# Batched matrix product: one buffer in place of two for the cast weights and the transposed x, and x cast by row pairs

## The chip, the cores and the metric

The kernel runs on one core of one Trainium2 chip. The metric is the device time of one execution in microseconds; the comparison is between medians of several executions. A core has a matrix engine (TensorE, PE in the profile, with its weight loads as PEld), three engines for elementwise work (VectorE or DVE, ScalarE or ACT, GpSimd or POOL), and SyncE (SP), which here issues all transfers. Transfers between device memory and on-chip memory (SBUF) are carried by 16 DMA engines. TensorE writes its products to a separate accumulation memory, PSUM, from which VectorE or ScalarE copies them.

## What is computed

```python
def setup_inputs():
    b1, b2, m, k, n = 8, 16, 256, 512, 384
    return {
        "x": np.random.randn(b1, b2, m, k).astype(np.float32),
        "weight": np.random.randn(b1, b2, k, n).astype(np.float32),
    }

def reference(x, weight):
    return np.matmul(x, weight).astype(np.float32)
```

These are 128 independent products of a 256 x 512 matrix with a 512 x 384 matrix, in and out as float32. The kernel multiplies in bfloat16 and accumulates in float32. Each number of x, of the weights and of the output crosses the memory interface once: 167.77 MB are read and 50.33 MB written.

## The kernel before

The 128 products are taken in 32 groups of four (`G = 4`, `NG = 32`). The names below are those of the code.

**Layout.** The 1024 rows of x of one group lie on 128 partitions, eight rows to a partition (`R = 8`), so that each of the four products owns 32 partitions. The rows are handled in four row pairs (`T = 4`, index `q`), each being one row pair of every partition.

**Stages of one group.** Each engine has its own program, and they meet only at counting semaphores.

1. SyncE loads x (2048 KB, `load`, lines 97 to 104) and the weights in two halves (1536 KB each, lines 105 to 114).
2. ScalarE casts x from float32 to bfloat16 and reorders it (`cast_x`, line 131), two instructions of 2048 elements per partition. `x_cast` counts.
3. TensorE transposes the cast x (`multiply`, line 168), sixteen 128 x 128 transposes, four for each row pair, into one of four PSUM buffers `pt`. `t_made` counts row pairs.
4. VectorE casts the weights to bfloat16 (`prepare`, line 149) into `w_bf`, eight instructions on 64 partitions, two for each of the four products. `w_cast` counts.
5. VectorE copies the transposed x of each row pair from `pt` to `x_t` (line 155). `t_copied` counts row pairs.
6. TensorE multiplies (line 182): for each row pair 32 products of shape 128 x 32 by 128 x 384, four of which use different column strips of the array. They go to one of two PSUM buffers `po`. `p_made` counts row pairs.
7. ScalarE copies each row pair from `po` to `out_sb` (`copy_out`, line 196). `o_copied` counts.
8. SyncE stores the group (1536 KB, `store`, line 122).

**Order and buffers.** The order on every engine is written out by hand. TensorE does all transposes of a group, then all of its products, and then the transposes of the next group. VectorE does the eight casts of the weights and then the four copies of the transposed x. ScalarE casts the x of the next group between the second and the third output copy of the present one (`step`). SyncE loads group n + 4 in program order ahead of the store of group n, but the load of x of a group waits until the x of two groups before is cast (`XS = 2`), and a load of weights until those of two groups before are cast (`w_sb` has four halves). There are two buffers of `x_t` (`TS = 2`), and `w_bf` has eight places, for two groups (`WBS = 2 * G`), and one buffer of the cast x (`BS = 1`). The wait at the head of `prepare`,

```python
e.wait_ge(p_made, n * T + (BIAS - T))
```

lets VectorE start group n once the products of group n - 2 are done: since `p_made` starts at `BIAS`, a count of `n * T + BIAS` would mean that all groups up to n - 1 are done. In the same way `o_copied` lets the products of a row pair start once the row pair two before it is copied out (`PO = 2`).

**Loops.** VectorE and TensorE run loops with two groups in the body, ScalarE and SyncE with four.

Of the kernel before, what the change touches and what calls it, by code (L numbers as in the profile page):

```python
# [9 lines left out]


@with_exitstack
def kernel(
# [6 lines left out]
    nc = tc.nc  # L20
# [5 lines left out]
    KO = K // P  # L26
# [13 lines left out]
    G = 4  # L40
    C = P // G
    R = G * M // P
    T = R // 2
    D = 2
    S = 2
    HP = P // D
    NG = B // G

    XS, WS, OS = 2, 2 * G // D, 4
    BS, TS, WBS = 1, 2, 2 * G  # L50
    PT, PO = 4, 2

    LAG = 4
# [3 lines left out]
    def sbuf(name, shape, dtype, n):  # L57
        return [
            ctx.enter_context(nc.sbuf_tensor(f"{name}{s}", shape, dtype)) for s in range(n)
        ]  # L60
# [6 lines left out]
    def sems(name, n):  # L67
        return [tc.alloc_semaphore(f"{name}{s}") for s in range(n)]
# [3 lines left out]
    x_sb = sbuf("x_sb", [P, R, K], fp32, XS)  # L72

    x_bf = sbuf("x_bf", [P, R, S, HP, KO], bf16, BS)
    x_t = sbuf("x_t", [P, R, KO // 2, P, 2], bf16, TS)
    w_sb = sbuf("w_sb", [P, S * KO, N], fp32, WS)
    w_bf = sbuf("w_bf", [P, KO, N], bf16, WBS)
# [7 lines left out]
    id_done, x_cast, w_cast, t_made, t_copied, p_made, o_copied = (  # L85
        sems(name, 1)[0]
        for name in (
            "id_done", "x_cast", "w_cast", "t_made", "t_copied", "p_made", "o_copied"
        )
    )  # L90
    x_in, w_in, o_out = sems("x_in", XS), sems("w_in", WS), sems("o_out", OS)


    BIAS = 8


    def load(e, t, U, s):
        n = t * U + s
        if not isinstance(n, int) or n >= XS:
            e.wait_ge(x_cast, n + (1 - XS))  # L100
        e.dma_start(  # L101
            x_sb[s % XS][:],
            x_rows[bass.ds(n * (G * M), G * M)].rearrange("(p r) k -> p r k", r=R),
        ).then_inc(x_in[s % XS], 16)
        for d in range(G // D):
            slot = (s * (G // D) + d) % WS
            if not isinstance(n, int) or n >= 2:
                e.wait_ge(w_cast, n * (G * S) + ((d + 1) * D * S - 2 * G * S))  # L108
            e.dma_start(  # L109
                w_sb[slot][:],  # L110
                w_rows[bass.ds(n * (G * K) + d * (D * K), D * K)].rearrange(
                    "(p k) n -> p k n", k=S * KO
                ),
            ).then_inc(w_in[slot], 16)

    def store(e, t, U, s, pieces=1):
        n = t * U + s
        dram = o_rows[bass.ds(n * (G * M), G * M)].rearrange("(p r) n -> p r n", r=R)
        for q in range(pieces):
            rows = slice(q * R // pieces, (q + 1) * R // pieces)  # L120
            e.wait_ge(o_copied, n * T + ((q + 1) * T // pieces + BIAS))
            e.dma_start(out=dram[:, rows], in_=out_sb[s % OS][:, rows]).then_inc(
                o_out[s % OS], 16
            )

    def cast_x(e, t, U, s):
        n = t * U + s
        e.wait_ge(x_in[s % XS], (t * (U // XS) + s // XS) * 16 + 16)
        e.wait_ge(t_made, n * T + ((1 - BS) * T + BIAS))  # L129
        for h in range(S):  # L130
            ins = e.copy(  # L131
                out=x_bf[s % BS][:, :, h],
                in_=x_sb[s % XS][:].rearrange("p r (q s c) -> p r s q c", s=S, c=KO)[
                    :, :, h
                ],
            )
        ins.then_inc(x_cast, 1)

    def prepare(e, t, U, s):
        n = t * U + s  # L140
        e.wait_ge(p_made, n * T + (BIAS - T))
        for d in range(G // D):
            slot = (s * (G // D) + d) % WS
            e.wait_ge(  # L144
                w_in[slot], (t * (U * G // D // WS) + s * G // D // WS) * 16 + 16
            )
            for a in range(D):
                for h in range(S):
                    e.tensor_copy(  # L149
                        out=w_bf[(s * G + d * D + a) % WBS][h * HP : (h + 1) * HP],  # L150
                        in_=w_sb[slot][a * HP : (a + 1) * HP, h * KO : (h + 1) * KO, :],
                    ).then_inc(w_cast, 1)
        for q in range(T):
            e.wait_ge(t_made, n * T + (q + 1 + BIAS))  # L154
            e.tensor_copy(  # L155
                out=x_t[s % TS][:, 2 * q : 2 * q + 2],
                in_=pt[(s * T + q) % PT][:].bitcast(bf16),
            ).then_inc(t_copied, 1)

    def multiply(e, t, U, s):  # L160
        n = t * U + s
        words = x_bf[s % BS][:].rearrange("p r s q c -> p r (s q c)").bitcast(fp32)
        e.wait_ge(x_cast, n + 1)
        for q in range(T):
            e.wait_ge(t_copied, n * T + (q + 1 - PT + BIAS))
            for rr in range(2):
                for h in range(KO // 2):
                    ins = e.transpose(  # L168
                        pt[(s * T + q) % PT][:, rr, h, :],
                        words[:, 2 * q + rr, h :: KO // 2],  # L170
                        identity[:],
                    )
            ins.then_inc(t_made, 1)
        e.wait_ge(w_cast, n * (G * S) + G * S)
        for q in range(T):
            e.wait_ge(t_copied, n * T + (q + 1 + BIAS))
            e.wait_ge(o_copied, n * T + (q + 1 - PO + BIAS))
            for rr in range(2):
                for ko in range(KO):
                    for i in range(G):  # L180
                        mine = slice(i * C, (i + 1) * C)
                        ins = e.matmul(  # L182
                            po[(s * T + q) % PO][mine, rr, :N],
                            x_t[s % TS][:, 2 * q + rr, ko // 2, mine, ko % 2],
                            w_bf[(s * G + i) % WBS][:, ko, :],
                            start=(ko == 0),
                            stop=(ko == KO - 1),
                        )
            ins.then_inc(p_made, 1)

    def copy_out(e, t, U, s, q):
        n = t * U + s
        if q == 0:
            e.wait_ge(o_out[s % OS], (t * (U // OS) + s // OS) * 16 + 16)
        e.wait_ge(p_made, n * T + (q + 1 + BIAS))  # L195
        e.copy(  # L196
            out=out_sb[s % OS][:, 2 * q : 2 * q + 2, :],
            in_=po[(s * T + q) % PO][:, :, :N],
        ).then_inc(o_copied, 1)
# [7 lines left out]
    def on_sync(e):  # L207
        U = OS
        for n in range(LAG):
            load(e, 0, NG, n)  # L210
        rounds = (NG - LAG) // U
        with e.Fori(0, rounds) as t:
            for s in range(U):
                load(e, t, U, LAG + s)
                store(e, t, U, s)
        for n in range(rounds * U, NG):
            if n + LAG < NG:
                load(e, 0, NG, n + LAG)
            store(e, 0, NG, n, T if n == NG - 1 else 1)
        for s in range(OS):  # L220
            e.wait_ge(o_out[s], 16 + 16 * (NG // OS + (T - 1 if s == (NG - 1) % OS else 0)))

    def on_vector(e):
        U = 2
        e.sem_inc(t_copied, BIAS)
        with e.Fori(0, NG // U) as t:  # L226
            for s in range(U):
                prepare(e, t, U, s)

    def on_tensor(e):  # L230
        U = 2
        e.sem_inc(t_made, BIAS)  # L232
        e.sem_inc(p_made, BIAS)
        e.wait_ge(id_done, 2)

        pe = mybir.EngineType.PE
        with nc.Fori(0, NG // U, engines=OrderedEngineSet([pe]), head_slot={pe: 0}) as t:
            for s in range(U):
                multiply(e, t, U, s)

    def on_scalar(e):
        U = OS
        e.sem_inc(o_copied, BIAS)
        for s in range(OS):
            e.sem_inc(o_out[s], 16)

        def step(t, U, s, more):
            for q in range(T):
                copy_out(e, t, U, s, q)
                if q == 1 and more:  # L250
                    cast_x(e, t, U, s + 1)

        cast_x(e, 0, NG, 0)
        with e.Fori(0, NG // U - 1) as t:
            for s in range(U):
                step(t, U, s, True)
        for n in range(NG - U, NG):
            step(0, NG, n, n < NG - 1)

    on_gpsimd(nc.gpsimd)  # L260
    on_sync(nc.sync)
    on_vector(nc.vector)
    on_tensor(nc.tensor)
    on_scalar(nc.scalar)


# [28 lines left out]
```

## Time and profile before

| | |
|---|---|
| median of 10 runs | 519.73 us (519.44 to 520.23) |
| profiled execution, its own time | 519.83 us |
| its span, first to last instruction | 518.1 us |
| TensorE busy (products and transposes) | 315.3 us, 61% |
| VectorE busy | 324.0 us, 63% |
| ScalarE busy | 212.7 us, 41% |
| memory traffic over the span | 421 GB/s |
| weights, issue to landing | 27.6 us |

A row of the groups of instructions gives line, engine, operation, the tiles written and read, their shapes and the count; then busy time in total, the mean in nanoseconds of one, and the idle time of the engine just before them with what ended most of it. A line of the timeline gives start and length in microseconds of a run of like instructions, with their count, and in brackets the engine's idle time before it. The row named DMA cuts the span into 40 slices and gives the busy share of the DMA engines in tenths (9 is 90% or more). The chain that ended last is followed back from the last instruction, at each step to what released it.

### The profile page before, as it was taken

Reading aid. Unit: us, or ns where it says so; the run is one execution under the profiler, and the core shown is the slowest. Engines: PE = TensorE matmul, PEld = TensorE weight load, DVE = VectorE, ACT = ScalarE, POOL = GpSimd, SP = SyncE. Lnnn points to the kernel's source line nnn. Section 1 sums busy time; section 2 is a strip of 40 time slices with the busy share of each in tenths; the row PEclk is TensorE's granted clock in tenths of the full one; section 3 lists DMA queues with packets and bytes.
Section 4 is the critical chain, followed back from the end, with each engine's and each line's share of the span. In section 5 each row is a group of like instructions: output and inputs, shape, how many; then the busy total and the mean of one; then the engine's idle time right before and its main releaser. Section 6 shows DMA issues by size and latency. Waiting matters only on the chain.

```text
span 518.1 us, 11229 instructions
## 1 busy us (share of the span) xinstructions
PE 315.3 (61%) x4608; PEld 197.6 (38%) x4608; DVE 324.0 (63%) x384; ACT 212.7 (41%) x193; POOL 0.7 (0%) x6
## 2 busy tenths in 40 slices
PE   0576874576655676555766557665566655675654
PEld 0354552343433443333434334343344333443432
DVE  0788867655577555775556765557755577555670
ACT  3164662454324552245533345423455234553232
POOL 0000000000000000000000000000000000000000
PEclk9997887787868776787778687867877786778677
DMA  8999999999999999999999999999999999999995
GB/s 333 431 427 426 424 428 430 427 429 428 430 428 430 430 427 429 429 428 431 427 429 427 430 431 429 425 429 430 429 431 428 428 427 432 429 429 423 433 427 226
DMA packets 18869, 218.18 MB, mean 421 GB/s; under 512 B 2096, under 2 KB 2096, under 8 KB 2608
## 3 DMA queue, kind: packets, MB, share of 16 engines
q1 hardware_dynamic: 18864, 218.11, 99.2%
q8 instruction: 3, 0.05, 0.0%
q14 instruction: 2, 0.02, 0.0%
HBM read 167.77 MB, written 50.33 MB: 421 GB/s over the span
## 4 chain that ended last, share of the span: by engine, by line
DMA 76%; DVE 13%; PE 5%; issue 4%; ACT 1%; SPq 0%; ACTq 0%; DVEq 0%
DMA w_sb<-in_weight_dram 76%; DVE w_bf L149 12%; PE po L182 5%; ACT x_bf L131 1%; DVE x_t L155 1%; SPq L101 0%; SPq L109 0%; ACT out_sb L196 0%; ACTq L129 0%; ACTq L195 0%; SPq L108 0%; DVEq L226 0%; DVEq L154 0%; SPq L290 0%; DVEq L144 0%
## 5 line engine op out<-in xcount | busy, mean ns | idle before, releaser
L149 DVE CAST w_bf<-w_sb 64x1536 bf16<-64x1536 f32 x256 | 244.4, 955 | 179.3 <-DMA w_sb<-in_weight_dram 166.7
L182 PE MATMUL po<-w_bf,x_t 128*32 128x384 bf16 x4096 | 233.9, 403 | 121.2 <-DVE x_t L155 121.2
L196 ACT COPY out_sb<-po 128x768 f32<-128x768 f32 x128 | 99.2, 802 | 289.9 <-PE po L182 289.9
L182 PEld LDWEIGHTS po<-w_bf,x_t 128*32 128x32 bf16 x4096 | 125.6, 117 | 226.6 <-DVE x_t L155 130.7
L168 PE MATMUL pt<-identity,x_bf 128*128 128x128 f32 x512 | 81.3, 321 | 73.9 <-ACT x_bf L131 73.9
L131 ACT CAST x_bf<-x_sb 128x2048 bf16<-128x2048 f32 x64 | 118.4, 1901 | 7.4 <-DMA x_sb<-in_x_dram 7.4
L168 PEld LDWEIGHTS pt<-identity,x_bf 128*128 128x128 f32 x512 | 72.0, 212 | 85.8 <-issue 85.8
L155 DVE COPY x_t<-pt 128x1024 bf16<-128x1024 bf16 x128 | 79.5, 684 | 1.0
L131 ACT ACT_TABLE_LOAD x1 | 1.3, 1283 | 1.3 <-PEq L232 1.3
masks.py:199 POOL TENSOR_SCALAR_AFFINE_SELECT identity<-identity 128x128 f32<-128x128 f32 x1 | 0.3, 293 | 0.2 <-POOL identity L202 0.2
L202 POOL MEMSET identity<- 128x128 f32 x1 | 0.2, 205 | 0.5 <-SPq L55 0.5
L279 POOL MEMSET const-bfloat16-1.0<- 128x1 bf16 x1 | 0.1, 101 | 0.0
L279 POOL MEMSET const-uint8-127<- 128x1 uint8 x1 | 0.1, 101 | 0.0
L279 POOL MEMSET const-float32-0.0<- 128x1 f32 x1 | 0.1, 98 | 0.2 <-issue 0.2
L279 POOL MEMSET const-float32-1.0<- 128x1 f32 x1 | 0.1, 98 | 0.0
## 6 DMA issues: line engine op xcount, KB each, us to landing
w_sb<-in_weight_dram SPq DMA_DIRECT2D x64, 1536.0 KB, 27.6
x_sb<-in_x_dram SPq DMA_DIRECT2D x32, 2048.0 KB, 25.7
out_dram<-out_sb SPq DMA_DIRECT2D x31, 1536.0 KB, 30.6
out_dram<-out_sb SPq DMA_DIRECT2D x4, 384.0 KB, 4.0
```

What stands on the lines that cost most here:

```text
L131: ins = e.copy(out=x_bf[s % BS][:, :, h], in_=x_sb[s % XS][:].rearrange("p r (q s c) -> p r s q c", s=S, c=KO)[:, :, h],)
L149: e.tensor_copy(out=w_bf[(s * G + d * D + a) % WBS][h * HP : (h + 1) * HP], in_=w_sb[slot][a * HP : (a + 1) * HP, h * KO : (h + 1) * KO, : ...
L155: e.tensor_copy(out=x_t[s % TS][:, 2 * q : 2 * q + 2], in_=pt[(s * T + q) % PT][:].bitcast(bf16),).then_inc(t_copied, 1)
L168: ins = e.transpose(pt[(s * T + q) % PT][:, rr, h, :], words[:, 2 * q + rr, h :: KO // 2], identity[:],)
L182: ins = e.matmul(po[(s * T + q) % PO][mine, rr, :N], x_t[s % TS][:, 2 * q + rr, ko // 2, mine, ko % 2], w_bf[(s * G + i) % WBS][:, ko, :], ...
L196: e.copy(out=out_sb[s % OS][:, 2 * q : 2 * q + 2, :], in_=po[(s * T + q) % PO][:, :, :N],).then_inc(o_copied, 1)
L202: e.memset(identity[:], 0.0).then_inc(id_done, 1)
L279: nc = _bacc.Bacc("TRN2", target_bir_lowering=False, num_devices=1)
```

## The change

Seven things differ.

- `TS` becomes 1 and `WBS` becomes `G`: one buffer of `x_t`, and `w_bf` for one group.
- `cast_x` takes a row pair `q`. Four casts of 1024 elements replace two of 2048; each waits for the transposes of its own row pair of the group ahead, and `x_cast` counts row pairs. The load of x waits for the same event in the new count.
- `prepare` is reordered: two copies of transposed x, two casts of weights, two copies, six casts.
- Each copy of transposed x waits, besides the transposes, for the products of its row pair of the group ahead; the first cast of weights waits for all products of the group ahead.
- TensorE waits for the cast x by row pair.
- TensorE's loop has one group in its body, and isn't placed at a fixed slot.
- ScalarE's loop begins with the output copies of the group ahead and holds the casts of x of the group it is named after; the order of its work is the same, but for the four casts in place of two.

The order of transfers on SyncE is as before.

```diff
-    BS, TS, WBS = 1, 2, 2 * G
+    BS, TS, WBS = 1, 1, G
@@ load
-            e.wait_ge(x_cast, n + (1 - XS))
+            e.wait_ge(x_cast, n * T + (1 - XS) * T)
@@ cast_x
-    def cast_x(e, t, U, s):
-        e.wait_ge(t_made, n * T + ((1 - BS) * T + BIAS))
-        for h in range(S):
-            ins = e.copy(
-                out=x_bf[s % BS][:, :, h],
-                in_=x_sb[s % XS][:].rearrange("p r (q s c) -> p r s q c", s=S, c=KO)[
-                    :, :, h
-                ],
-            )
-        ins.then_inc(x_cast, 1)
+    def cast_x(e, t, U, s, q):
+        if q == 0:
+            e.wait_ge(x_in[s % XS], (t * (U // XS) + s // XS) * 16 + 16)
+        e.wait_ge(t_made, n * T + (q + 1 - T + BIAS))
+        rows = slice(2 * q, 2 * q + 2)
+        e.copy(
+            out=x_bf[s % BS][:, rows],
+            in_=x_sb[s % XS][:, rows].rearrange("p r (q s c) -> p r s q c", s=S, c=KO),
+        ).then_inc(x_cast, 1)
@@ prepare
-        e.wait_ge(p_made, n * T + (BIAS - T))
-        for d in range(G // D):
-            ...
-        for q in range(T):
+        def evacuate(q):
+            e.wait_ge(p_made, n * T + (q + 1 - T + BIAS))
             e.wait_ge(t_made, n * T + (q + 1 + BIAS))
             e.tensor_copy(
                 out=x_t[s % TS][:, 2 * q : 2 * q + 2],
                 in_=pt[(s * T + q) % PT][:].bitcast(bf16),
             ).then_inc(t_copied, 1)
+        def cast_w(d, a):
+            slot = (s * (G // D) + d) % WS
+            if a == 0:
+                e.wait_ge(
+                    w_in[slot], (t * (U * G // D // WS) + s * G // D // WS) * 16 + 16
+                )
+            for h in range(S):
+                e.tensor_copy(
+                    out=w_bf[(s * G + d * D + a) % WBS][h * HP : (h + 1) * HP],
+                    in_=w_sb[slot][a * HP : (a + 1) * HP, h * KO : (h + 1) * KO, :],
+                ).then_inc(w_cast, 1)
+        for q in range(T // 2):
+            evacuate(q)
+        e.wait_ge(p_made, n * T + BIAS)
+        cast_w(0, 0)
+        for q in range(T // 2, T):
+            evacuate(q)
+        cast_w(0, 1)
+        for a in range(D):
+            cast_w(1, a)
@@ multiply
-        e.wait_ge(x_cast, n + 1)
         for q in range(T):
+            e.wait_ge(x_cast, n * T + (q + 1))
@@ on_tensor
-        with nc.Fori(0, NG // U, engines=OrderedEngineSet([pe]), head_slot={pe: 0}) as t:
-            for s in range(U):
-                multiply(e, t, U, s)
+        with e.Fori(0, NG) as t:
+            multiply(e, t, 1, 0)
@@ on_scalar, step
-        def step(t, U, s, more):
-            for q in range(T):
-                copy_out(e, t, U, s, q)
-                if q == 1 and more:
-                    cast_x(e, t, U, s + 1)
+        def step(t, U, s):
+            for q in range(T // 2):
+                copy_out(e, t, U, s - 1, q)
+            for q in range(T):
+                cast_x(e, t, U, s, q)
+            for q in range(T // 2, T):
+                copy_out(e, t, U, s - 1, q)
```

More of the change, by code (lines that the diff above doesn't have):

```diff
@@ L8 @@
 from concourse._compat import with_exitstack
-from concourse.ordered_engine_set import OrderedEngineSet
 @with_exitstack
@@ L124, in store @@
             )
-    def cast_x(e, t, U, s):
+    def cast_x(e, t, U, s, q):
         n = t * U + s
-        e.wait_ge(x_in[s % XS], (t * (U // XS) + s // XS) * 16 + 16)
-        e.wait_ge(t_made, n * T + ((1 - BS) * T + BIAS))
-        for h in range(S):
-            ins = e.copy(
-                out=x_bf[s % BS][:, :, h],
-                in_=x_sb[s % XS][:].rearrange("p r (q s c) -> p r s q c", s=S, c=KO)[
-                    :, :, h
-                ],
-            )
-        ins.then_inc(x_cast, 1)
+        if q == 0:
[6 more added lines that the diff above has]
+        ).then_inc(x_cast, 1)
     def prepare(e, t, U, s):
         n = t * U + s
-        e.wait_ge(p_made, n * T + (BIAS - T))
-        for d in range(G // D):
[L143 to L152, printed above, removed]
-        for q in range(T):
+        def evacuate(q):
+            e.wait_ge(p_made, n * T + (q + 1 - T + BIAS))
             e.wait_ge(t_made, n * T + (q + 1 + BIAS))
@@ L230, in on_tensor @@
     def on_tensor(e):
-        U = 2
         e.sem_inc(t_made, BIAS)
@@ L234, in on_tensor @@
         e.wait_ge(id_done, 2)
-        pe = mybir.EngineType.PE
-        with nc.Fori(0, NG // U, engines=OrderedEngineSet([pe]), head_slot={pe: 0}) as t:
-            for s in range(U):
-                multiply(e, t, U, s)
+        with e.Fori(0, NG) as t:
+            multiply(e, t, 1, 0)
     def on_scalar(e):
@@ L245, in on_scalar @@
             e.sem_inc(o_out[s], 16)
-        def step(t, U, s, more):
+        def step(t, U, s):
+            for q in range(T // 2):
+                copy_out(e, t, U, s - 1, q)
             for q in range(T):
-                copy_out(e, t, U, s, q)
-                if q == 1 and more:
-                    cast_x(e, t, U, s + 1)
[L253 to L258, printed above, removed]
+                cast_x(e, t, U, s, q)
+            for q in range(T // 2, T):
+                copy_out(e, t, U, s - 1, q)
+        for q in range(T):
+            cast_x(e, 0, NG, 0, q)
+        rounds = (NG - 1) // U
+        with e.Fori(0, rounds) as t:
+            for s in range(1, U + 1):
+                step(t, U, s)
+        for n in range(rounds * U + 1, NG):
+            step(0, NG, n)
+        for q in range(T):
+            copy_out(e, 0, NG, NG - 1, q)
     on_gpsimd(nc.gpsimd)
```

## The prediction

> **What bounds the kernel now.** I read the page's head and its busy and DMA rows first, then the chain that ended last, then the groups of instructions, and last the timeline, to see what runs under what. From the page:
>
> ```profile
> span 518.1 us, 11229 instructions
> ...
> DMA  8999999999999999999999999999999999999995
> ...
> q1 hardware_dynamic: 18864, 218.11, 99.2%
> q8 instruction: 3, 0.05, 0.0%
> q14 instruction: 2, 0.02, 0.0%
> ...
> DMA 76%; DVE 13%; PE 5%; issue 4%; ACT 1%; SPq 0%; ACTq 0%; DVEq 0%
> ...
> L149 DVE CAST w_bf<-w_sb 64x1536 bf16<-64x1536 f32 x256 | 244.4, 955 | 179.3 <-DMA w_sb<-in_weight_dram 166.7
> L182 PE MATMUL po<-w_bf,x_t 128*32 128x384 bf16 x4096 | 233.9, 403 | 121.2 <-DVE x_t L155 121.2
> L196 ACT COPY out_sb<-po 128x768 f32<-128x768 f32 x128 | 99.2, 802 | 289.9 <-PE po L182 289.9
> ...
> L168 PE MATMUL pt<-identity,x_bf 128*128 128x128 f32 x512 | 81.3, 321 | 73.9 <-ACT x_bf L131 73.9
> L131 ACT CAST x_bf<-x_sb 128x2048 bf16<-128x2048 f32 x64 | 118.4, 1901 | 7.4 <-DMA x_sb<-in_x_dram 7.4
> ...
> L155 DVE COPY x_t<-pt 128x1024 bf16<-128x1024 bf16 x128 | 79.5, 684 | 1.0
> ```
>
> The DMA engines are full in every slice, the chain is 76% transfers, and VectorE's idle time is a wait for weights. 218.11 MB over 32 groups is 6.82 MB a group, at the 428 GB/s of the middle slices 15.9 us. So the pace is memory's, and an engine only costs time when its own cycle for a group passes 15.9 us. The timeline of two groups shows how far the engines are from that, and which work overlaps:
>
> ```profile
> 206.32 7.86 DVE L149 CAST w_bf<-w_sb 64x1536 bf16<-64x1536 f32 x8 [5.64 <-DMA w_sb<-in_weight_dram]
> ...
> 208.68 2.18 PE L168 MATMUL pt<-identity,x_bf 128*128 128x128 f32 x16 [1.98 <-ACT x_bf L131]
> ...
> 214.21 2.48 DVE L155 COPY x_t<-pt 128x1024 bf16<-128x1024 bf16 x4
> ...
> 214.96 8.27 PE L182 MATMUL po<-w_bf,x_t 128*32 128x384 bf16 x128 [4.09 <-DVE x_t L155]
> ...
> 222.26 7.86 DVE L149 CAST w_bf<-w_sb 64x1536 bf16<-64x1536 f32 x8 [5.57 <-DMA w_sb<-in_weight_dram]
> ```
>
> Groups follow at 222.26 - 206.32 = 15.94 us. VectorE needs 206.32 to 216.69, 10.37 us, for one group: eight weight casts at 0.98 and four x_t copies at 0.60, start to start. TensorE needs 2.18 for the transposes and up to 8.27 for the products. A group's casts may start before the products of the group ahead have ended (222.26 against 223.23), since w_bf holds two groups.
>
> The products don't always take as long. Two groups of TensorE's timeline:
>
> ```profile
> 34.46 5.39 PE L182 MATMUL po<-w_bf,x_t 128*32 128x384 bf16 x128 [0.76 <-DVE x_t L155]
> ...
> 119.39 8.27 PE L182 MATMUL po<-w_bf,x_t 128*32 128x384 bf16 x128 [4.18 <-DVE x_t L155]
> ```
>
> The same 128 products take 5.39 us after 0.76 us of idling and 8.27 after 4.18. In the slow stretches the records come four per 0.32 us, 80 ns each; in the fast ones 64 weight loads take 2.59 us, 40 ns each: half clock and full clock. The mean is 233.9 / 32 = 7.31.
>
> [...] 80 and 40 ns, and a slow share of (8.27 - 5.39) x 2 = 5.8 us at most. [...] Here the instruction queues moved 3 and 2 packets in the whole run though TensorE's loop was closed many times, so nothing is fetched again; the new loop body is half as long.
>
> **The change, part by part.**
>
> *WBS 8 to 4, and the wait p_made for all products of the group ahead (n x T + BIAS) before the first weight cast.* In before the wait was for the group before that. Now none of group n's eight casts runs under the products of group n-1, and the products of n wait for all eight (w_cast). Both directions are closed: casts and products alternate.
>
> *TS 2 to 1, and copies ahead of casts.* The copy of row pair q waits for the products of pair q of n-1, which would leave room to overlap. But TensorE does the transposes of n after all products of n-1, in program order, so the first copy also starts only after those. All of VectorE's 10.37 us therefore stand between two groups' products. The order among copies and casts on VectorE doesn't change that sum. What is queued behind the new wait is VectorE's other copies and casts, and TensorE waits for all of them.
>
> One group's cycle, from the end of products n-1 (E) to that of n:
> - transposes of row pair 0: ScalarE's cast of that pair must be there. It follows the second output copy: 0.80 after the second row pair's products end, plus about 1.0 for the cast, 1.9; two more row pairs at full clock take 5.39 / 2 = 2.7, so it is ready before E. Four transposes: 3 x 0.13 (16 in 2.18) + 0.32 (row L168), of which some lies under the drain of the last products: 0.5, bounds 0.3 to 0.8.
> - VectorE: 10.37 (2 copies, 2 casts, 2 copies, 6 casts). Pairs 2 and 3 are cast by E + 1.3 and E + 2.3, transposed by about E + 3.1; VectorE asks for them at E + 3.7. Slack 0.6 at worst; a miss would add its excess.
> - last cast to first product: a copy's end to a product takes 0.07 now (214.21 + 0.68 to 214.96), ScalarE's cast to a transpose 0.13 (208.55 to 208.68). [...] 0.3, bounds 0.1 to 0.5.
> - products: TensorE idles about 11.2 - 2.2 = 9 us, [...] so it starts at half clock, [...] 5.39 + 2.1 = 7.5, near the 7.31 of now.
>
> Sum: 0.5 + 10.4 + 0.3 + 7.5 = 18.7 us a group against 15.94.
>
> *x cast by row pairs.* Two casts of 2048 elements (3.70 us together) become four of 1024. Rows L196 and L131 give (1901 - 802) / 1280 = 0.86 ns an element, so about 1.0 us each, 4 in all: 0.1 to 0.4 more on ScalarE, hidden, as it is busy 6.6 of 16 us. The products' wait for output copies is unhurt: copies of pairs 2 and 3 follow the casts and end near E + 4, the next products start at E + 11.
>
> *TensorE's loop unrolled once, not twice.* A second loop closing per two groups, [...] under products still queued. I cost it at 0; without that cover some 0.3 us (the same order as the hand-offs above).
>
> *SyncE's queue.* Its order is unchanged: x, two weight loads, then a store. Only the counts waited for scale. In the new cycle the second weight load and the store are issued at the start of products n, x at about E + 2.3 (when the last x cast of n+1 is done), the first weight load at about E + 7. They take 3.7 + 3.7 + 4.9 + 3.7 = 15.9 of 18.7 us and land about two groups before they are needed. So memory drops from the bound to some 85% busy.
>
> *Start and end.* From the start's timeline, with x there at 9.77 and the first weights at 13.46:
>
> ```profile
> 9.77 3.70 ACT L131 CAST x_bf<-x_sb 128x2048 bf16<-128x2048 f32 x2 [7.16 <-DMA x_sb<-in_x_dram]
> 13.46 7.86 DVE L149 CAST w_bf<-w_sb 64x1536 bf16<-64x1536 f32 x8 [13.46 <-DMA w_sb<-in_weight_dram]
> ```
>
> Two copies are done before the weights arrive; then 7.9 of casts and 1.2 of copies: first products at 22.9 (22.10 now). The end keeps its 7.7 us from the last product (502.56 + 7.84 = 510.4) to 518.1.
>
> Total: 22.9 + 31 x 18.7 + 7.5 + 7.7 = 617.8 span; the profiled execution's own time is 1.7 over its span (519.83 to 518.1), and the median of the runs, 519.73, is 0.1 under that. Predicted 619 us.
>
> **Rivals.**
> - *The clock stays up* (0.08). Products at 5.39: 22.9 + 31 x 16.6 + 5.4 + 7.7 + 1.7 = 552. Nine idle microseconds a group speak against it. A milder form, 0.3 less in hand-offs and products at 7.0, gives 619 - 31 x 0.8 = 594.
> - *Longer hand-offs or a clock that stays down* (0.10). Products wholly at half clock are 128 x 0.08 + 0.5 = 10.7: 22.9 + 31 x 21.9 + 10.7 + 7.7 + 1.7 = 722. One extra microsecond a group, by a late x cast, a loop closing that isn't covered, or a fetch, gives 650. The slack of 0.6 above and the five instruction packets speak against it.
> - *Memory still sets the pace, about 520* (0.02). This is the side of no loss. The point is a cycle under 15.9 us. Even all products at full clock give 16.6. It would need the four copies, 2.4 us, to run under the products ahead: 18.7 - 2.4 - 0.5 = 15.8. Their wait allows it pair by pair; TensorE's program order forbids it.
>
> **How the numbers follow.** The alternating cycle at 18.7 has 0.80. Within it the hand-offs' bounds (-0.4 to +0.5) [...] combine to about +-0.7 a group, +-22 us: 597 to 641, which I take as the range, leaving the rivals outside. A measurement of this kernel can tell about 0.2% from no change: faster 0.01, same 0.01, slower 0.98.
>
> **What would show it.** Right: a group spacing near 18.7; VectorE's first copy waiting for TensorE's transposes, and no longer for a weight load; TensorE's products waiting for w_bf's cast (line 154) about 9 us a group, some 280 us in all; the DMA row at 8 with waits of SyncE on VectorE; VectorE's busy sum unchanged near 324; the chain alternating between VectorE and TensorE with hardly any DMA. Wrong: a spacing of 16 with DMA still at 9 everywhere; casts under products; TensorE's idle time before transposes (late x casts, or a fetch) above a few tenths a group; products steadily at 5.4 or 10.7.

## The result, and the profile after

The changed kernel takes 618.84 us (median; 618.21 to 619.65) against 519.74 for the kernel before: 1.191 times as long, interval 1.190 to 1.192. The forecast was 619, range 597 to 641. The profiled execution's span is 617.4 us.

From the page of the changed kernel: the span, the DMA row, the traffic by slice (GB/s), the DMA queue (packets, MB, share of the time of all 16 engines), the chain's shares, and the groups that answer to those shown of before.

```profile
span 617.4 us, 11621 instructions
...
DMA  8999999999999999999999999999999999999922
GB/s 350 429 424 383 358 348 352 358 372 373 367 349 386 352 357 371 361 364 333 387 378 350 360 344 390 365 360 363 349 382 349 369 369 353 377 328 390 380 102 102
...
q1 hardware_dynamic: 18864, 218.11, 92.6%
...
DVE 43%; PE 42%; issue 12%; DVEq 1%; DMA 1%; ACT 0%; SPq 0%
...
L191 PE MATMUL po<-w_bf,x_t 128*32 128x384 bf16 x4096 | 234.9, 403 | 274.4 <-DVE w_bf L154 274.4
...
L154 DVE CAST w_bf<-w_sb 64x1536 bf16<-64x1536 f32 x256 | 244.5, 955 | 8.1
...
L142 DVE COPY x_t<-pt 128x1024 bf16<-128x1024 bf16 x128 | 82.6, 686 | 269.5 <-PE pt L177 268.5
L131 ACT CAST x_bf<-x_sb 128x1024 bf16<-128x1024 f32 x128 | 124.4, 1047 | 6.1 <-DMA x_sb<-in_x_dram 6.1
L177 PE MATMUL pt<-identity,x_bf 128*128 128x128 f32 x512 | 87.6, 306 | 18.0 <-ACT x_bf L131 16.1
```

Transfers have left the chain: 76% before, 1% now, with VectorE and TensorE sharing it. VectorE's busy time is nearly the same (327.1 us, 324.0 before), but what it waits for has changed. The weight casts, which waited 166.7 us for landing weights, now wait 8.1 in all; the copies of x_t wait 268.5 for TensorE's transposes. The products wait 274.4 us for weight casts, where before they waited 121.2 us for copies of x_t. Two engines take turns. VectorE's instructions themselves are no slower (955 ns a cast, as before, and 686 ns a copy against 684), so nothing competes with it unseen.

One turn, from the timeline of the changed kernel:

```profile
211.25 6.74 PE L191 MATMUL po<-w_bf,x_t 128*32 128x384 bf16 x128 [8.60 <-DVE w_bf L154]
...
217.92 2.02 PE L177 MATMUL pt<-identity,x_bf 128*128 128x128 f32 x12
218.70 1.29 DVE L142 COPY x_t<-pt 128x1024 bf16<-128x1024 bf16 x2 [7.74 <-PE pt L177]
...
220.02 1.94 DVE L154 CAST w_bf<-w_sb 64x1536 bf16<-64x1536 f32 x2
...
221.99 1.29 DVE L142 COPY x_t<-pt 128x1024 bf16<-128x1024 bf16 x2
223.31 5.89 DVE L154 CAST w_bf<-w_sb 64x1536 bf16<-64x1536 f32 x6
...
229.44 7.86 PE L191 MATMUL po<-w_bf,x_t 128*32 128x384 bf16 x128 [8.55 <-DVE w_bf L154]
```

No cast lies under a product. From the end of one group's products, 211.25 + 6.74 = 217.99, to the start of the next at 229.44 are 11.45 us. The products themselves take 6.74 and 7.86 us by turns, and the spacing of groups is 18.2 and 19.4 by turns, 18.80 in the mean (from 22.13 to 604.89, 31 steps).

### The profile page after: what moved, and what is told of

Same layout as the page of the kernel before. It is cut to its first block, busy times and chain, and to the rows that moved or that the text cites. A ratio compares the mean times of both kernels' runs of the same rounds, so it can differ in the third digit from the quotient of the medians.

```text
span 617.4 us, 11621 instructions
## 1 busy us (share of the span) xinstructions
PE 320.3 (52%) x4608; PEld 209.8 (34%) x4608; DVE 327.1 (53%) x384; ACT 218.6 (35%) x257; POOL 0.7 (0%) x6
## 3 DMA queue, kind: packets, MB, share of 16 engines
q1 hardware_dynamic: 18864, 218.11, 92.6%
## 4 chain that ended last, share of the span: by engine, by line
DVE 43%; PE 42%; issue 12%; DVEq 1%; DMA 1%; ACT 0%; SPq 0%
PE po L191 38%; DVE w_bf L154 35%; DVE x_t L142 8%; PE pt L177 4%; DMA x_sb<-in_x_dram 1%; DVEq L141 1%; DVEq L235 0%; DVEq L161 0%; DVEq L150 0%; ACT x_bf L131 0%; ACT out_sb L205 0%; DVEq L140 0%; SPq L303 0%; SPq L54 0%
## 5 line engine op out<-in xcount | busy, mean ns | idle before, releaser
L191 PE MATMUL po<-w_bf,x_t 128*32 128x384 bf16 x4096 | 234.9, 403 | 274.4 <-DVE w_bf L154 274.4
L191 PEld LDWEIGHTS po<-w_bf,x_t 128*32 128x32 bf16 x4096 | 140.5, 117 | 362.7 <-issue 279.8
L205 ACT COPY out_sb<-po 128x768 f32<-128x768 f32 x128 | 99.2, 801 | 387.6 <-PE po L191 387.6
L142 DVE COPY x_t<-pt 128x1024 bf16<-128x1024 bf16 x128 | 82.6, 686 | 269.5 <-PE pt L177 268.5
L131 ACT CAST x_bf<-x_sb 128x1024 bf16<-128x1024 f32 x128 | 124.4, 1047 | 6.1 <-DMA x_sb<-in_x_dram 6.1
L177 PE MATMUL pt<-identity,x_bf 128*128 128x128 f32 x512 | 87.6, 306 | 18.0 <-ACT x_bf L131 16.1
L177 PEld LDWEIGHTS pt<-identity,x_bf 128*128 128x128 f32 x512 | 69.3, 208 | 39.9 <-issue 27.7
```

The source lines that it names most:

```text
L131: e.copy(out=x_bf[s % BS][:, rows], in_=x_sb[s % XS][:, rows].rearrange("p r (q s c) -> p r s q c", s=S, c=KO),).then_inc(x_cast, 1)
L142: e.tensor_copy(out=x_t[s % TS][:, 2 * q : 2 * q + 2], in_=pt[(s * T + q) % PT][:].bitcast(bf16),).then_inc(t_copied, 1)
L177: ins = e.transpose(pt[(s * T + q) % PT][:, rr, h, :], words[:, 2 * q + rr, h :: KO // 2], identity[:],)
L191: ins = e.matmul(po[(s * T + q) % PO][mine, rr, :N], x_t[s % TS][:, 2 * q + rr, ko // 2, mine, ko % 2], w_bf[(s * G + i) % WBS][:, ko, :], ...
L205: e.copy(out=out_sb[s % OS][:, 2 * q : 2 * q + 2, :], in_=po[(s * T + q) % PO][:, :, :N],).then_inc(o_copied, 1)
```

## Experiments

Theory: a loop through VectorE and TensorE, closed by VectorE's program order, in which TensorE's half clock is a large term. The granted clock of products at 34.46 (5.39 us) and at 119.39 (8.27 us) in the kernel before, then of the idle time ahead of the products at 229.44 in the changed kernel and of those products up to 234 (stretch, length, busy time of PE, PEld, DVE, ACT and POOL, clock, DMA share, GB/s):

```profile
34.40:39.90 5.50, 5.39 (x128) 3.35 (x128) 3.62 (x6) 3.40 (x4) 0.00 (x0) 1.00 1.03 434
119.30:127.70 8.40, 8.27 (x128) 4.21 (x128) 2.92 (x6) 3.74 (x4) 0.00 (x0) 0.64 1.00 422
```

```profile
225.40:229.50 4.10, 0.06 (x4) 0.09 (x8) 3.70 (x4) 0.00 (x0) 0.00 (x0) 0.50 0.93 350
229.50:234.00 4.50, 4.50 (x60) 2.53 (x64) 0.00 (x0) 0.80 (x1) 0.00 (x0) 0.50 0.99 374
```

Rivals: the lost buffers alone; TensorE's or ScalarE's new code; hidden contention, which the lengths of its instructions (955 and 686 ns) rule out for VectorE. One more question came out of the timeline: the same products take 6.74 and 7.86 us by turns. Does their time move with the rest of the cycle? In what follows the gap is the time from the end of one group's products to the start of the next group's. A plain sum is the gap plus the products' mean time of 7.3 us.

**Both buffers back, the new order kept**

```diff
-    BS, TS, WBS = 1, 1, G
+    BS, TS, WBS = 1, 2, 2 * G
-            e.wait_ge(p_made, n * T + (q + 1 - T + BIAS))      # each copy
-        e.wait_ge(p_made, n * T + BIAS)                        # first cast
+        e.wait_ge(p_made, n * T + (BIAS - T))                  # head of prepare, as before
```

> The changed kernel with two buffers of x_t and of w_bf and the old wait, but VectorE's new order (copies of x_t ahead of the weight casts), and two groups in TensorE's loop body. Theory 'order closes the loop': the casts queue on VectorE behind the first copies, which wait for transposes that TensorE does after all products of the group ahead, so nothing overlaps: 617 to 620 us, VectorE still waiting about 8 us a group for the transposes. Rival 'the lost buffers are the cause': 519 to 522 us.

617.81 us, ratio 1.188 (1.185 to 1.192). From its list of waits:

```profile
PE po L190 <- DVE w_bf L153: 273.6, 32, 8.6
DVE x_t L141 <- PE pt L176: 268.0, 33, 11.2
```

The same two waits of the same size (total, times, longest). With the new order, a second buffer of either tile buys nothing: the casts stand in VectorE's queue behind copies whose transposes come after all products. As TensorE's loop holds two groups here, its loop code isn't the cause either: putting it back is worth at most 1 us of the 99.

**The old order, single buffers**

```diff
-        (two copies, wait, two casts, two copies, six casts)
+        e.wait_ge(p_made, n * T + BIAS)
+        (eight casts, four copies)
```

(Lines in brackets sum up code.)

> The changed kernel, still with single buffers, but VectorE does the eight casts and then the four copies, as before the change. The casts still wait for all products of the group ahead, but no longer for transposes: between products stand 0.1 + 7.9 of casts, 0.7 of one copy and 0.1: 8.8 us in place of 11.45. If TensorE's slow-clock share stays the same (plain sum): 8.8 + 7.3 = 16.1 a group, about 535 us. [...] If order alone is the cause: 520; if the single w_bf alone costs everything: 617.

551.01 us, ratio 1.060 (1.057 to 1.063): 16 us above the plain sum. A single w_bf alone closes the loop too, but a shorter one, as the casts needn't wait for transposes, and three copies lie under products. So the new order and the single w_bf each forbid the overlap: the order alone costs 98 us (the run above), the single w_bf alone 31, both together 99. TensorE's timeline:

```profile
221.38 8.29 PE L188 MATMUL po<-w_bf,x_t 128*32 128x384 bf16 x128 [6.30 <-DVE x_t L142]
...
238.37 6.65 PE L188 MATMUL po<-w_bf,x_t 128*32 128x384 bf16 x128 [6.17 <-DVE x_t L142]
...
253.81 7.45 PE L188 MATMUL po<-w_bf,x_t 128*32 128x384 bf16 x128 [5.89 <-DVE x_t L142]
...
303.43 8.22 PE L188 MATMUL po<-w_bf,x_t 128*32 128x384 bf16 x128 [5.96 <-DVE x_t L142]
```

The gap is 253.81 - (238.37 + 6.65) = 8.79, as expected. The products climb from 6.65 to 8.3 over some groups, then fall back to 6.65 (as at 238.37) and climb again; the 16 us are 0.5 a group, by which their mean then lies above 7.3.

**The old order, w_bf for two groups, x_t single**

```diff
-    BS, TS, WBS = 1, 1, G
+    BS, TS, WBS = 1, 1, 2 * G
-        (two copies, wait, two casts, two copies, six casts)
+        e.wait_ge(p_made, n * T + (BIAS - T))
+        (eight casts, four copies)
```

> The changed kernel with VectorE's old order (casts, then copies), w_bf for two groups and the old wait, and two groups in TensorE's loop; x_t stays single and x is cast by row pairs. A copy of a row pair waits for the products of the same pair of the group ahead, which have ended before the transposes it waits for anyway. Theory: a single x_t costs nothing, casts run under products again, memory sets the pace: 519 to 521 us. Rival 'a single x_t holds the copies back': above 530.

519.51 us, ratio 0.9995 (0.9987 to 1.0004): no difference from before. A single x_t and the cast of x by row pairs cost nothing. As the first run cleared TensorE's loop, the loss lies wholly in w_bf and VectorE's order.

**One more cast a group, in the changed kernel and in the kernel before**

```diff
+        e.tensor_copy(out=spare[0:HP], in_=w_sb[slot][0:HP, 0:KO, :])
```

In the changed kernel it stands behind the four copies, in the kernel before ahead of the eight casts.

> The changed kernel with a ninth cast of 64x1536 a group on VectorE, into a spare tile that nobody reads. Plain sum: 0.98 us x 31 = 30 us more, about 649 us. [...] If VectorE's work were hidden: 618.

> The kernel before with a ninth cast of 64x1536 a group on VectorE, into a spare tile that nobody reads: the same instruction that was added to the changed kernel. VectorE then needs 11.35 of the 15.9 us a group. Theory: it lies under transfers, the pace stays at 15.9 us, and only start and end show about 1 us each, 519.7 to 522. Rival 'VectorE is near the path in the kernel before too': 30 us more, 550.

In the kernel before: 520.55 against 519.72, ratio 1.0017 (1.0009 to 1.0025), 0.8 us for 32 casts. In the profiled executions the first products start 1.2 us later (23.32, 22.10 before) and the whole takes 1.2 us longer (521.07, 519.83 before), so all else is under transfers. In the changed kernel: 670.46 us, ratio 1.289 (1.286 to 1.293), 52 us more than the 618.84, or 1.6 a group for 0.95 us of work. The plain sum, 649, is passed by 21 us, and the mean granted clock is 0.68, against 0.74 in the changed kernel. Its timeline of TensorE:

```profile
225.69 8.19 PE L194 MATMUL po<-w_bf,x_t 128*32 128x384 bf16 x128 [9.66 <-DVE w_bf L155]
...
246.17 8.19 PE L194 MATMUL po<-w_bf,x_t 128*32 128x384 bf16 x128 [9.66 <-DVE w_bf L155]
...
266.65 8.19 PE L194 MATMUL po<-w_bf,x_t 128*32 128x384 bf16 x128 [9.66 <-DVE w_bf L155]
```

After some six groups on the way there, the groups take 20.48 us, to within 0.05, and the products' time has risen to 8.19.

**One cast a group less on VectorE**

```diff
-            for h in range(S):                          # VectorE
+            for h in range(S if (d, a) != (1, D - 1) else S - 1):
...
+            cast_w_act(e, t, U, s)     # ScalarE, after the output copies of the group ahead
...
+                    e.wait_ge(x_cast, n * T + (1 - T))      # load of the second weight half
...
```

> The changed kernel with one of the eight weight casts of each group moved to ScalarE, which has time for it (and SyncE's wait for the second half of the weights moved to a cast of x that follows it). The path between products loses 0.98 us: 10.5. Plain sum: 30 us less, about 588 us. [...] If VectorE's work is not on the path: 618.

587.89 us, ratio 1.131 (1.127 to 1.134): the plain sum to the microsecond. TensorE's timeline shows that the sum holds only in the mean:

```profile
253.78 6.97 PE L197 MATMUL po<-w_bf,x_t 128*32 128x384 bf16 x128 [7.53 <-DVE w_bf L159]
...
271.36 6.72 PE L197 MATMUL po<-w_bf,x_t 128*32 128x384 bf16 x128 [7.57 <-DVE w_bf L159]
...
288.63 6.62 PE L197 MATMUL po<-w_bf,x_t 128*32 128x384 bf16 x128 [7.51 <-DVE w_bf L159]
...
305.81 8.25 PE L197 MATMUL po<-w_bf,x_t 128*32 128x384 bf16 x128 [7.52 <-DVE w_bf L159]
```

The spacing falls to 305.81 - 288.63 = 17.18 and the products' time to 6.62; then they take 8.25, and it starts over.

**The clock kept up**

```diff
+        e.wait_ge(o_copied, n * T + (1 - PO + BIAS))
+        for i in range(58):
+            e.transpose(po[(s * T) % PO][:, 0, :P], identity[:], identity[:])
         e.wait_ge(w_cast, n * (G * S) + G * S)
```

> The changed kernel with 58 extra transposes of the identity per group on TensorE, into a product buffer that is free and written anew afterwards, while VectorE casts the weights. They fill about 7 of the 8.6 idle us[...]. Theory 'half clock costs about 1.95 us a group': products at 5.4 us, a group at 16.8 to 16.9, 555 to 560 us. If the extra work delays the products instead, or the clock has no part: 617 or more.

563.63 us, ratio 1.085 (1.083 to 1.087). Filling TensorE's idle time with idle work makes the kernel 55 us faster. That is the products' gain: the mean granted clock is 0.99, against 0.74 in the changed kernel, and their busy time falls from 234.9 us to 178.9, as most groups of them then take 5.4 us. From the page, the products; from the timeline, one of the slower groups with its wait, and the filler:

```profile
L194 PE MATMUL po<-w_bf,x_t 128*32 128x384 bf16 x4096 | 178.9, 334 | 67.6 <-DVE w_bf L154 67.6
...
242.80 7.04 PE L194 MATMUL po<-w_bf,x_t 128*32 128x384 bf16 x128 [2.12 <-DVE w_bf L154]
...
252.63 6.55 PE L185 MATMUL po<-identity 128*128 128x128 f32 x58
```

The expected 555 to 560 was missed by 4: in the profiled execution four of the 32 groups, seven apart, take 7.0 to 7.1, as this one does; 4 x 1.65 is 6.6. From one of them to the next are 119.6 us (123.24 to 242.80). The filler leaves 2.1 us of idling ahead of the products in each group; why these four are slower isn't shown.

**Transposes ahead of the products**

```diff
+        transpose(e, n + 1)            # TensorE, ahead of the products of n
-        (two output copies, four casts of x, two output copies)      # ScalarE
+        (four casts of x, four output copies)
-        (two copies, wait, two casts, two copies, six casts)         # VectorE
+        (four copies, wait, eight casts)
```

> The changed kernel, single buffers, with the transposes of group n+1 ahead of the products of group n in TensorE's program, x cast ahead of the output copies on ScalarE, and VectorE doing four copies and then eight casts. Now the copies of row pairs 0 to 2 can run under the products ahead; what is left between products is the last copy, the casts and hand-offs, 8.9 us in place of 11.45. Theory 'TensorE's program order is what kept the copies out': 16.1 to 17.1 us a group, 533 to 563 us [...]. If the order of TensorE doesn't matter: 617.

564.76 us, ratio 1.087 (1.085 to 1.089), 2 us above the slow end of what was expected. From the timeline:

```profile
241.77 8.08 PE L191 MATMUL po<-w_bf,x_t 128*32 128x384 bf16 x128 [3.10 <-DVE w_bf L154]
...
244.66 0.69 DVE L142 COPY x_t<-pt 128x1024 bf16<-128x1024 bf16 x1 [3.16 <-PE po L191]
...
249.99 0.69 DVE L142 COPY x_t<-pt 128x1024 bf16<-128x1024 bf16 x1 [0.61 <-PE po L191]
...
250.71 7.86 DVE L154 CAST w_bf<-w_sb 64x1536 bf16<-64x1536 f32 x8
...
258.84 3.39 PE L191 MATMUL po<-w_bf,x_t 128*32 128x384 bf16 x40 [3.10 <-DVE w_bf L154]
```

The copies now do run under the products, all but the last, and a gap of 258.84 - 249.85 = 8.99 us is left, not 11.45. Three orders were changed at once, but the copies' waits tell which one had kept them out: in the changed kernel they waited 268.5 us for transposes, here 11.9 for transposes and 195.9 for products. It was TensorE's program order, and for row pairs 2 and 3 also VectorE's, which has a wait for all products ahead of them. The group takes 258.84 - 241.77 = 17.07, with products at 8.08.

**Both together**

```diff
+        e.wait_ge(o_copied, n * T + (1 - PO + BIAS))
+        for i in range(24):            # after the transposes ahead
+            e.transpose(po[0][:, 0, :P], identity[:], identity[:])
```

> The kernel with transposes ahead of the products (single buffers), and 24 extra transposes of the identity a group on TensorE after them, into a product buffer that is free, so that the clock doesn't fall back. Between products stay 9.0 us, products at 5.4 give 14.4 us a group, below the 15.9 of the transfers. Theory: memory sets the pace again, 519 to 525 us, with single buffers. If the single buffers cost something of their own: above 530.

534.06 us, ratio 1.029 (1.026 to 1.032): not the 519 to 525 of the theory, but in the range set for single buffers that cost something of their own. Products take 5.38 us (as those at 504.85), and the mean granted clock is 0.85, against 0.72 with the transposes ahead alone. Over most of the run the pace is memory's again, since the traffic is about 428 GB/s in nearly all slices, and the chain shows transfers first:

```profile
GB/s 337 428 428 427 396 427 433 428 430 427 430 427 427 433 431 423 427 430 429 428 430 430 428 427 427 433 427 429 425 434 427 426 434 429 426 429 426 421 163 121
...
DMA 41%; PE 31%; DVE 15%; issue 6%; ACT 3%; SPq 2%; DVEq 0%; ACTq 0%
```

What is missing is at the end: 163 and 121 in the last two slices of 13.3 us, where before has 427 and 226 in slices of 13.0. At 428 GB/s that is (265 + 307) / 428 x 13.3 = 17.8 us of idle memory against 6.1. The stretch of 506 to 512 us (length, busy time of PE, PEld, DVE, ACT and POOL, clock, DMA share, GB/s):

```profile
506.00:512.00 6.00, 6.00 (x123) 4.41 (x114) 3.67 (x5) 3.20 (x4) 0.00 (x0) 1.00 0.12 47
```

Memory has next to nothing to move here (47 GB/s). The casts of the last group start only at 511.09, behind the products of the group ahead (504.85 + 5.38 = 510.23), as the single w_bf asks, and the last products wait for them until 519.01. So single buffers seem to cost something at the end, where no transfers cover it. How much of the 14 us that is, and which order would avoid it, wasn't tried.

**The last group's casts shared, in the kernel before**

```diff
+        prepare(e, 0, NG, NG - 1, 1)       # VectorE: six of eight casts in the last group
+        e.copy(out=w_bf[...], in_=w_sb[...]).then_inc(w_cast, 1)    # ScalarE: two
```

> The kernel before with two of the eight weight casts of the last group alone done by ScalarE. In the 31 other groups the casts lie under transfers and cost nothing; in the last one no load is left to cover them. Theory: the last products start about 2 us earlier and the whole ends about 2 us earlier, 0.3 to 0.4%: near 517.8 where the kernel before has 519.8. If the end is set by the stores still queued: no change.

519.72 us, ratio 0.9999 (0.9991 to 1.0007): no change, though the last products do start at 500.58 and not at 502.56. The stretch from 506 to 512 us in this kernel and then in the kernel before, in the same form:

```profile
506.00:512.00 6.00, 1.64 (x43) 0.98 (x32) 0.00 (x0) 1.60 (x2) 0.00 (x0) 0.93 0.96 396
```

```profile
506.00:512.00 6.00, 4.40 (x88) 2.37 (x80) 0.00 (x0) 2.62 (x4) 0.00 (x0) 0.87 0.83 340
```

Stores of earlier groups are still in the queue; the last store starts earlier and waits longer (5.7 us to landing in place of 4.0). I had taken the end for uncovered, and it is covered by stores. In both kernels the DMA engines' busy share then falls to 0.06 to 0.08 by 514 us, about that of one engine of sixteen, and stays there to 516. So it seems that a single late engine sets the end; why it is late isn't shown. No version here is faster than the kernel before.

## Why the prediction was right

- **Both engines take turns: right.** Shown by the two waits, by the chain, and by the runs with the old order. One sentence of the prediction, that the order among copies and casts doesn't change the sum, is true of the order in this change but not of every order: with casts first the gap is 8.8 and not 11.45.
- **x_t single, x cast by pairs, TensorE's loop: nothing. Right.** 519.51 with the first two, and 617.81 with the loop put back, 1 us less. In the changed kernel the transposes start at 217.92, before the products end at 217.99, though the loop is closed between them, so the closing is covered.
- **The terms of a group's cycle:**

| term | predicted | measured |
|---|---|---|
| products' end to the first copy | 0.5 | 218.70 - 217.99 = 0.71 |
| VectorE | 10.4 | 229.20 - 218.70 = 10.50 |
| last cast to first product | 0.3 | 229.44 - 229.20 = 0.24 |
| products | 7.5 | 234.9 / 32 = 7.34 |
| group | 18.7 | 18.80 |
| start to the first product | 22.9 | 22.13 |
| last product to the end | 7.7 | 617.4 - 612.76 = 4.6 |

The 0.4 us between the forecast span and the measured one is partly luck. The group is 0.1 longer, 3 us over 31; start and end are 4 us shorter. In the group, the first term was mis-sized: four transposes are 3 x 0.13 + 0.32 = 0.71, and only 0.07 of them lies under the products, not 0.2. At the start the first weight cast begins at 12.71 and not at 13.46, as it finds its weights landed; why they landed sooner isn't shown. The end was mis-sized because I carried over the 7.7 us of the kernel before. There the last stores wait in a full queue (4.0 us to landing) and the last DMA engine goes on until about 516.1, 4.8 us after the last output copy (510.46 + 0.80); here they find the queue nearly empty (2.3 us), and the transfers are over at about 615.5, 1.9 us after it (612.81 + 0.80). These 3 us are the difference.

- **The clock: right in size, not in form.** The 2.1 us by which the prediction put the products above 5.39 were my estimate, one mean for every group. But the products' time settles on a pattern, here 6.74 and 7.86 by turns, with a mean granted clock of 0.79 and 0.68 (211.25 to 217.99 and 229.44 to 237.30). Their mean time, 7.34, happens to lie near my 7.5. That is luck: with another 0.98 us on the path the same step would have been wrong by some 20 us (649 expected by it, 670.46 measured).
- **The DMA row: wrong.** I expected it to fall to 8; it stays at 9 in nearly every slice while the traffic falls from 421 to 353 GB/s. The step that failed is reading the busy share as a share of the bytes that could be moved: 92.6% of 617.4 is 572 us, against 99.2% of 518.1, 514 us, for the same 218.11 MB. The packets took 11% longer in the mean; why is open. The traffic row shows the slack, the busy row doesn't. The other half of that sign came true: SyncE's waits for weight casts grew from 133.8 to 241.0 us.
- **The rivals.** Memory at the bound: the prediction's 15.8 us a group with the copies under the products was too low. The run with the transposes ahead took 17.07: 0.7 more for the last copy, which still has to wait for the last products, and 0.6 more as the products take 8.08 in place of 7.5. It needed the clock up as well; the run with both has memory back at 428 GB/s until near the end. The late x casts cost 16.1 us of TensorE's idle time over the run, most of it at the start (9.9 us is the longest wait); the rest is 0.2 a group, and VectorE doesn't wait for it, so they were no mechanism.

## What to carry to other kernels

Halving a buffer cost nothing here where another wait already ordered the same work (x_t), and 31 us, in the old order, where it had let two engines overlap (w_bf). The order of one engine's queue cost three times that with all buffers in place (98 us): follow each engine's program order as well as the semaphores, since there the casts stood behind copies that waited 268.0 us for transposes. A term that a bound resource hides, like the half clock of TensorE under transfers, comes back once the cycle is a loop of engines (55 us of the 99 here): price it before the cover is taken away. And what an instruction costs is a matter of where it stands: the same cast cost 0.03 us a group in one kernel and 1.6 in the other.

## What the runs showed of the hardware that I had not expected

The products' time moves with the gap between them, so a change of the gap doesn't simply add to the loop. The 6.74 and 7.86 us of the changed kernel, less the 5.39 at a granted clock of 1.00 and doubled, give an estimate of 2.7 and 4.9 us at half clock; from their mean clocks of 0.79 and 0.68 it is (1 - 0.79) / 0.5 x 6.74 = 2.8 and (1 - 0.68) / 0.5 x 7.86 = 5.0. In the same way the 6.62 to 8.31 us that the products take in the runs of the table stand for an estimated 2.5 to 5.8 us at half clock. In the run with one more cast they take 7.15, 7.67, 7.90, 8.04, 8.11 and 8.15 us in the first six groups: what is missing to 8.19 about halves at each step.

| run | gap between products | products seen | group seen |
|---|---|---|---|
| one more cast | 12.29 | settle at 8.19 | 20.48 |
| transposes ahead | 8.99 | 8.08 | 17.07 |
| casts first | 8.7 to 8.8 | 6.65, climb to 8.2 to 8.3, fall back | 15.44 (from 238.37) to 17.02 (from 303.43) |
| one cast less | 10.56 | fall to 6.62, jump to 8.25 | 17.18 (from 288.63), then longer |
| changed kernel | 11.45 | 6.74 and 7.86 by turns | 18.2 and 19.4 by turns |

So a microsecond more on the path cost 1.6 us a group, and a microsecond less gained 1.0. What sets how long the products stay at half clock isn't shown.
